# A top-k search by bits: comparison with a constant, update by columns, one more block counted on ScalarE, reciprocals by pairs

## The chip, the cores and the metric

The kernel runs on one core of one Trainium2 chip. The metric is device microseconds from start to end of the program, as the median of repeated runs. PE is TensorE, the matrix engine; PEld is its weight load; DVE is VectorE, ACT is ScalarE, POOL is GpSimd, SP is SyncE, which here issues DMAs. Each engine works off its own instructions in a fixed order, and an instruction that waits for another engine holds up everything behind it on its own.

## The reference, cut to what matters

One decoder layer on 1024 tokens of width 1024, in float32: a feed-forward part (FFN1), a mixer, a second feed-forward part (FFN2), each followed by a LayerNorm. The change lies in the mixer, above all in the choice of the 256 keys of each query:

```python
def block(i):                      # 128 queries, Q_BLOCK * i + 0..127
    causal = key_pos[None, :] <= t[:, None]
    logit = einsum('bqhd,bsd->bqhs', qib, ki_f) * IDX_DIM ** -0.5
    score = einsum('bqh,bqhs->bqs', wib, relu(logit))
    score = where(causal[None], score, -inf)
    _, sel = lax.top_k(score, 256)
    ...
    sc = einsum('bqhc,bqkc->bqhk', qa, c[sel])
    p = softmax(where(valid, sc, -inf), axis=-1)
    o_lat = einsum('bqhk,bqkc->bqhc', p, c[sel])
```

Beside the attention the mixer has a gated MLP (gelu of a projection, a LayerNorm of one half, a 128x128 spatial matrix for each of 8 groups, a product with the other half), and one output projection over both.

## The kernel before

Every product of float32 operands is made of three matmuls: each operand is split into a high part (an ACT copy, L87) and the remainder (a subtraction on DVE or POOL, L88), and `mm3` (L112 to L114) adds high times high, high times low and low times high.

The stages of the mixer, in the order of PE: the projection of the indexer's keys and queries and of a first piece of columns (`piece`, tiles `pN`), with the indexer's scores between them (`scores`, tile `lg`: ACT takes the relu at L758, DVE adds the four heads); two more pieces whose gelus ACT writes into `v` and `u` (L1090, L1096); the gate (`gate`, tile `sv`, DVE L895); transposes of the gated part and its output projection (`wout`, tile `y`); query projections (`queries`, tile `pT`, evacuated by ACT L662, L663 and DVE L664 into `ql`); `q_abs` (tile `qa`, evacuated by L87 on ACT and L88 on DVE, some by L94 and L96); and the attention, block by block of 128 queries: `softmax` (tile `sc`) and, one job later, `attend` (transposes, tile `pT`, tile `ol`).

Which keys are allowed is found for every query without sorting. `topk` finds the 256th largest score of each row bit by bit: 31 steps, each of which sets a trial bit, counts how many scores of the row lie below the trial value, and keeps or drops the bit. Blocks 0 and 1 need no search. A first search runs for blocks 3 and 2 together (two columns in the small tiles), a second one for blocks 7, 5, 4 and 6 (four columns, in this order). In a step, one block's row of scores is counted by one instruction: on ACT (L798, the sign of score minus trial, summed) or on DVE (L789). A comparison of the sums with a row of limits (L801), the next value from the comparison's result (L810) and the next trial bit (L808) follow on DVE, in 128x2 or 128x4 values. The sums on ACT and DVE count differently, so the limits are a small tile with one constant for each column (memsets at L785). In the first search ACT counts block 3 (512 scores) and DVE block 2 (384); in the second ACT counts blocks 7 and 5 (1024 and 768) and DVE blocks 4 and 6 (640 and 896). After the last step come an adjustment of the ACT blocks (L816 to L828, which counts them once on DVE) and, block by block, the mask: ACT counts once more (L839), POOL writes a mask (L844), DVE finds equal scores and their rank (L848 to L854), POOL adds them (L855).

Both searches are generators in a list of background work. `pump(n)` takes n steps of every generator there; the calls stand between the pieces, the projections and the attention's jobs, with the numbers of a table (P0, PX, B, C, Q, W, A). That gives the order of the program; a scheduler of the framework then orders each engine's instructions by a timeline that it estimates itself. `attention` pumps until the mask of a block is there before it begins that block.

`softmax` adds the mask and finds the maximum on DVE (L964, `m`), takes the exponential on ACT (L966), which also sums it into a 128x1 tile `l`, takes the reciprocal on DVE (L967), and multiplies on POOL (L968). Two heads share a tile `p`.

The page of `score` for block 4 (640 of 1024 columns) also holds block 2's 384 columns.

## Time and profile before

| | |
|---|---|
| Median of three runs | 1787.45 us (1786.04, 1787.45, 1789.47) |
| The profiled execution | 1789.27 us, of which the span is 1787.6 us |
| Granted TensorE clock, mean of that execution | 0.989 |
| Busy share of the span: PE, DVE, ACT, POOL | 97%, 74%, 44%, 25% |
| The first search: first and last count on DVE of both searches | 692.9 us, 915.2 us |
| The first and the last softmax reciprocal | 924.4 us, 1059.0 us |

The profile shows one execution, with times in microseconds from the start of the span. "PE busy" counts the stretch of the matmuls at whatever clock was granted, so a stage can be slow either because PE is idle or because its granted clock is below 1.00; the clock has two levels, 1.2 and 2.4 GHz, and a number between stands for a mix of both. A bracket at a row's end, as in [2.71 <-ACT u L1096], is the idle time of that engine before that instruction and what ended it.

### The profile page before, as it was taken

To read this page: it belongs to the slowest core of one execution; us is meant where nothing else is said; L and a number is where in the kernel's file an instruction comes from. 1 tells how busy PE (TensorE), PEld (TensorE's weight loads), DVE (VectorE), ACT (ScalarE), POOL (GpSimd) and SP (SyncE) were. 2 spreads that over 40 slices of the span, in tenths; PEclk is the share of its full clock that TensorE was granted. 3 is DMA by queue.
4 is the path that set the end of the run, shared out by engine and by line. 5 is a ranking of instruction groups with operands and counts; after the bars stand their busy time and mean duration, and the time that the engine had idled before them with its cause. 6 is when DMAs were issued, how large, how long until landed. Compare 5 with 4: busy or idle time off the path is not lost.

```text
span 1787.6 us, 22197 instructions
## 1 busy us (share of the span) xinstructions
PE 1734.7 (97%) x8056; PEld 1457.2 (82%) x8056; DVE 1322.2 (74%) x2186; ACT 787.5 (44%) x1328; POOL 453.0 (25%) x314
## 2 busy tenths in 40 slices
PE   8999999999999999998988999999999999999997
PEld 6878888888888889996867888888788888888886
DVE  5777755666885866899989877878777555589586
ACT  5421322323645336658796662453223222355551
POOL 0003422221000571224247430100323222200036
PEclk9999999999999999999999999999999999999999
DMA  7435432228554331113510005434453322763532
GB/s 284 154 135 200 157 126 88 89 103 310 181 169 138 124 118 43 48 48 103 176 46 25 1 1 195 170 118 169 162 182 119 140 94 89 274 198 124 182 100 83
DMA packets 81789, 235.36 MB, mean 132 GB/s; under 512 B 8208, under 2 KB 8720, under 8 KB 81680
## 3 DMA queue, kind: packets, MB, share of 16 engines
q1 hardware_dynamic: 78320, 225.82, 36.3%
q0 software_dynamic: 1920, 2.89, 0.8%
q10 hardware_dynamic: 1440, 5.24, 0.7%
q8 instruction: 63, 1.03, 0.2%
q14 instruction: 46, 0.38, 0.1%
HBM read 168.64 MB, written 62.39 MB: 129 GB/s over the span
## 4 chain that ended last, share of the span: by engine, by line
PE 82%; DVE 10%; ACT 3%; DMA 2%; issue 1%; POOL 1%; SPq 0%; ACTq 0%; POOLq 0%; DVEq 0%
PE ab L112 15%; PE ab L114 14%; PE ab L113 14%; PE y L112 5%; PE y L114 5%; PE y L113 5%; PE z L114 3%; PE z L112 3%; PE z L113 3%; DMA w<-in_ffn_w_dram 2%; PE tr L977 2%; DVE dve L789 1%; PE pN L112 1%; PE pN L114 1%; PE pN L113 1%
## 5 line engine op out<-in xcount | busy, mean ns | idle before, releaser
L112 PE MATMUL ab<-xs,hi 128*128 128x512 f32 x1232 | 481.7, 391 | 13.1 <-ACT xs L87 5.4
L113 PE MATMUL ab<-xs,hi 128*128 128x512 f32 x1232 | 480.8, 390 | 0.0
L114 PE MATMUL ab<-xs,lo 128*128 128x512 f32 x1232 | 480.6, 390 | 0.0
L112 PEld LDWEIGHTS ab<-xs,hi 128*128 128x128 f32 x1232 | 232.5, 189 | 62.5 <-ACT xs L87 5.4
L88 POOL TENSOR_TENSOR lo<-w,hi 128x1024 fp32r<-128x1024 f32 x54 | 136.8, 2534 | 565.1 <-ACT hi L87 508.0
L113 PEld LDWEIGHTS ab<-xs,hi 128*128 128x128 f32 x1232 | 232.6, 189 | 48.7 <-DVE xs L88 0.4
L114 PEld LDWEIGHTS ab<-xs,lo 128*128 128x128 f32 x1232 | 232.3, 189 | 48.4
L87 ACT ACTIVATE hi<-w 128x1024 fp32r<-128x1024 f32 (+1 forms) x134 | 137.1, 1039 | 184.7 <-DVE w L251 156.2
L88 DVE TENSOR_TENSOR lo<-w,hi 128x1024 fp32r<-128x1024 f32 (+1 forms) x80 | 94.8, 1195 | 42.3 <-ACT hi L87 41.6
L88 DVE TENSOR_TENSOR a<-hid,a 128x512 fp32r<-128x512 f32 x132 | 93.8, 711 | 25.3 <-ACT a L87 25.2
L307 ACT ACTIVATE h<-c 128x512 f32<-128x512 f32 x34 | 21.5, 631 | 202.2 <-DVE c L374 141.3
L87 ACT ACTIVATE a<-hid 128x512 fp32r<-128x512 f32 x132 | 82.0, 621 | 53.0 <-DMA hid<-f 49.8
L798 ACT ACTIVATE act<-score,tk 128x768 int8<-128x768 f32 (+2 forms) x93 | 86.8, 934 | 39.4 <-DVE tk L810 32.7
L88 DVE TENSOR_TENSOR b<-w,b 128x512 fp32r<-128x512 f32 x110 | 77.5, 704 | 34.2 <-ACT b L87 34.1
L113 PE MATMUL y<-b,a 128*128 128x512 f32 x264 | 102.7, 389 | 0.0
L114 PE MATMUL y<-b,a 128*128 128x512 f32 x264 | 102.7, 389 | 0.0
L113 PE MATMUL z<-b,a 128*128 128x512 f32 x264 | 102.7, 389 | 0.0
L114 PE MATMUL z<-b,a 128*128 128x512 f32 x264 | 102.7, 389 | 0.0
L112 PE MATMUL z<-b,a 128*128 128x512 f32 x264 | 102.5, 389 | 0.0
L112 PE MATMUL y<-b,a 128*128 128x512 f32 x264 | 102.0, 389 | 0.0
L551 POOL TENSOR_TENSOR xacc<-xacc,T 128x512 f32<-128x512 f32 x8 | 13.0, 1651 | 333.8 <-DVE T L524 333.8
L87 ACT ACTIVATE b<-w 128x512 fp32r<-128x512 f32 x110 | 68.4, 622 | 51.8 <-PE z L114 38.5
(272 smaller groups left out, 3657.5 us busy)
## 6 DMA issues: line engine op xcount, KB each, us to landing
w<-in_ffn_w_dram SPq DMA_DIRECT2D x110, 512.0 KB, 6.0
hid<-f SPq DMA_DIRECT2D x60, 512.0 KB, 3.7
w<-in_ffn_w_dram SPq DMA_DIRECT2D x22, 1024.0 KB, 11.2
f<-h SPq DMA_DIRECT2D x32, 512.0 KB, 3.4
f<-c SPq DMA_DIRECT2D x22, 512.0 KB, 3.0
xr<-x_spill SPq DMA_DIRECT2D x16, 512.0 KB, 4.9
x_spill<-xr SPq DMA_DIRECT2D x16, 512.0 KB, 2.9
f<-u SPq DMA_DIRECT2D x24, 256.0 KB, 3.7
```

Of the source, the lines that this page charges most:

```text
L87: nc.scalar.activation(hi, src, AF.Copy)
L88: (eng or nc.vector).tensor_tensor(lo, src, hi.bitcast(F32), ALU.subtract)
L112: mm(out, a[0], b[0], start=start, stop=False, skip_group_check=skip)
L113: mm(out, a[0], b[1], start=False, stop=False, skip_group_check=skip)
L114: mm(out, a[1], b[0], start=False, stop=stop, skip_group_check=skip)
L307: nc.scalar.activation(t, c[:, 0], AF.Silu)
L551: nc.gpsimd.tensor_tensor(acc[j][:, HALF:], acc[j][:, HALF:], T[j], ALU.add)
L789: V.tensor_scalar(self.marks("dve", s.shape[-1]), s, f, None, ALU.is_lt, ALU.add, accum_out=val[:, j : j + 1])
L798: nc.scalar.activation(out, s, AF.Sign, bias=fj, scale=-1.0, accum_out=val[:, j : j + 1])
L977: nc.tensor.transpose(pt[:, hh * P : (hh + 1) * P], ps4[hh][:, j * P : (j + 1) * P], self.ident)
```

## The change

- In the first search ACT counts both blocks, and block 2's scores are padded from 384 to 512 columns with -3e38, so that the two sums have the same limit. They lie in the second half of the page of block 3. DVE counts nothing in these steps.
- In the second search ACT still counts blocks 7 and 5, and block 5 is padded from 768 to 1024; DVE counts blocks 4 and 6 as before. DVE's counts begin from a constant that makes their sums comparable with ACT's.
- So there is one limit for all columns, and the comparison (L801, now L799) is a tensor_scalar with an immediate in place of a tensor_tensor with a tile. The tiles of limits and their six memsets are gone; two POOL memsets write the padding.
- The update (L810) was one scalar_tensor_tensor over two or four columns. It is now one tensor_scalar for each column, with the other operand as the column's scalar.
- Reciprocals are taken for two heads at once (128x2), after the second of them, and both heads are then multiplied on POOL one after the other. There are 32 of them in place of 64.

The table of pumps is the same.

```diff
-        dst = self.score[i]
+        dst = self.score[i][:, :s]
...
-    def topk(self, blocks, plan):
+    def topk(self, blocks, n_act):
...
-        for n, thr in zip(range(lo, n_act + 1), limits):
-            for j, i in enumerate(blocks):
-                nc.gpsimd.memset(thr[:, j : j + 1], float((i + 1) * P - (512 if j < n else 256)))
+        limit = float(self.score[blocks[0]].shape[-1] - 512)
 
         def below(f, j):
+
             s = self.score[blocks[j]]
-            V.tensor_scalar(self.marks("dve", s.shape[-1]), s, f, None, ALU.is_lt, ALU.add, accum_out=val[:, j : j + 1])
-
-        def count(f, n):
+            n = s.shape[-1]
+            V.tensor_scalar(self.marks("dve", n), s, f, limit - (n - 256), ALU.is_lt, ALU.add, accum_out=val[:, j : j + 1])
+
+        def count(f):
...
-                if j < n:
+                if j < n_act:
...
-            V.tensor_tensor(di, val, limits[n - lo], ALU.is_gt)
-
-        count(None, plan(31))
+            V.tensor_scalar(di, val, limit, None, ALU.is_gt)
+
+        count(None)
...
-            count(fa, plan(b))
-            V.scalar_tensor_tensor(fb.bitcast(I32), di, b, fni, ALU.logical_shift_left, ALU.bitwise_xor)
+            count(fa)
+            for j in range(w):
+                c = slice(j, j + 1)
+                V.tensor_scalar(fb.bitcast(I32)[:, c], di[:, c], b, fni[:, c], ALU.logical_shift_left, ALU.bitwise_xor)
...
-            if lo < n_act:
-                V.tensor_scalar(val[:, :lo], val[:, :lo], -256.0, None, ALU.add)
-                V.tensor_tensor(di[:, c], val[:, c], limits[0][:, c], ALU.is_le)
-            else:
-                V.tensor_scalar(val[:, c], val[:, c], -256.0, None, ALU.add)
-                V.tensor_tensor(di[:, c], val[:, c], limits[0][:, c], ALU.is_le)
+            V.tensor_scalar(di[:, c], val[:, c], limit, None, ALU.is_le)
...
-        m, l = self.small("m", 1), self.small("l", 1)
+        e = head % 2
+        if e == 0:
+            self.pp, self.sums = self.large("p", (P, 2, 1024), F32), self.small("l", 2)
+        p = self.pp[:, e]
+        m = self.small("m", 1)
...
-        nc.scalar.activation(p, p, AF.Exp, bias=m, scale=-1.0, accum_out=l)
-        V.reciprocal(l, l)
-        self.engine(PAR["PN"][head % 4]).tensor_scalar(p, p, l, 0.0, ALU.mult, ALU.add)
+        nc.scalar.activation(p, p, AF.Exp, bias=m, scale=-1.0, accum_out=self.sums[:, e : e + 1])
+        if e:
+            V.reciprocal(self.sums, self.sums)
+            for j in range(2):
+                x = self.pp[:, j, :s]
+                nc.gpsimd.tensor_scalar(x, x, self.sums[:, j : j + 1], 0.0, ALU.mult, ALU.add)
...
-        self.score = {7: pg[0], 6: pg[1][:, :896], 5: pg[2][:, :768], 4: pg[3][:, :640], 2: pg[3][:, 640:], 3: pg[4][:, :512]}
+        self.score = {7: pg[0], 6: pg[1][:, :896], 5: pg[2], 4: pg[3][:, :640], 2: pg[4][:, HALF:], 3: pg[4][:, :HALF]}
+        for i in (2, 5):
+            nc.gpsimd.memset(self.score[i][:, (i + 1) * P :], -3.0e38)
...
-            self.bg[:] = [self.topk([3, 2], lambda b: PAR["K1"][sum(b < x for x in PAR["K1B"])])]
+            self.bg[:] = [self.topk([3, 2], 2)]
...
-        self.bg.append(self.topk(PAR["KO"], lambda b: PAR["K2"][sum(b < x for x in PAR["K2B"])]))
+        self.bg.append(self.topk(PAR["KO"], 2))
```

The order of the instructions moves with it, at three places. The tiles `tk_...` are the small tiles of a search, and `score_...` is a block's scores; the numbers behind the names only number the tiles.

The first is DVE in the first search, at the end of the indexer's projections. Before, a step is a count of 384, the comparison, the update and the next trial bit:

```order
L808 TENSOR_SCALAR tk_5121<-tk_5117 128x2
L789 TENSOR_SCALAR dve_5207,tk_5116<-score_4749,tk_5117 128x384
L801 TENSOR_TENSOR tk_5119<-tk_5116,tk_5123 128x2
L810 SCALAR_TENSOR_TENSOR tk_5118<-tk_5119,tk_5121 128x2
L808 TENSOR_SCALAR tk_5121<-tk_5118 128x2
```

With the change:

```order
L664 TENSOR_TENSOR qil_4768<-pT_5175,qi_4764 128x512
L799 TENSOR_SCALAR tk_5121<-tk_5118 128x2
L810 TENSOR_SCALAR tk_5120<-tk_5121,tk_5123 128x1 x2
L806 TENSOR_SCALAR tk_5123<-tk_5120 128x2
L799 TENSOR_SCALAR tk_5121<-tk_5118 128x2
```

The count is gone from DVE, and each step is now four small instructions, of which the first waits for two counts on ACT.

The second place is ACT around the gelus of the last piece (`u<-pN`), before the gate. Before, the counts of the two searches (512, and 1024 with 768) stand between the gelus:

```order
L798 ACTIVATE act_6474,tk_5116<-score_4750,tk_5118 128x512
L1096 ACTIVATE u_5585<-pN_6095 128x384
L1096 ACTIVATE u_5586<-pN_6121 128x384
L798 ACTIVATE act_6481,tk_5889<-score_4746,tk_5890 128x1024
L798 ACTIVATE act_6483,tk_5889<-score_4748,tk_5890 128x768
L798 ACTIVATE act_6492,tk_5116<-score_4750,tk_5117 128x512
L1096 ACTIVATE u_5586<-pN_6147 128x384
L798 ACTIVATE act_6499,tk_5889<-score_4746,tk_5891 128x1024
```

With the change:

```order
L1097 ACTIVATE u_5601<-pN_6140 128x384
L796 ACTIVATE act_6509,tk_5905<-score_4746,tk_5906 128x1024
L1097 ACTIVATE u_5601<-pN_6166 128x384
L796 ACTIVATE act_6511,tk_5905<-score_4748,tk_5906 128x1024
L796 ACTIVATE act_6523,tk_5118<-score_4750,tk_5119 128x512
L796 ACTIVATE act_6525,tk_5118<-score_4750,tk_5119 128x512
L796 ACTIVATE act_6531,tk_5905<-score_4746,tk_5907 128x1024
L796 ACTIVATE act_6533,tk_5905<-score_4748,tk_5907 128x1024
L1097 ACTIVATE u_5602<-pN_6240 128x384
```

One gelu stands behind three counts before (1024, 768, 512), and behind five with the change.

The third is DVE where the attention begins. Before, the last step of the second search is over before the first softmax. With the change DVE has there:

```order
L799 TENSOR_SCALAR tk_5908<-tk_5905 128x4
L960 ISA p_7620,m_7629<-sc_7625,bias 128x256
L960 ISA m_7629 128x1
L88 TENSOR_TENSOR act_4481<-qa_7534,act_4480 128x4x128
L810 TENSOR_SCALAR tk_5906<-tk_5908,tk_5910 128x1 x4
L960 ISA p_7681,m_7683<-sc_7677,bias 128x256
L960 ISA m_7683 128x1
L964 RECIPROCAL l_7602<-l_7602 128x2
L787 TENSOR_SCALAR dve_7668,tk_5905<-score_4749,tk_5906 128x640
L960 ISA p_7681,m_7690<-sc_7686,bias 128x256
L960 ISA m_7690 128x1
L806 TENSOR_SCALAR tk_5910<-tk_5906 128x4
```

The steps of the second search now stand among the softmax sums (L960, `m`) and the evacuations of `qa`; ACT has eleven counts of 1024 between the split of `c` into `ch` and the first softmax of block 2, where before it had one count of 768 and four of the masks' counts.

## Rows read from the trace of the kernel before

**Rows 1.** The page: the span, and TensorE's busy time in it.

```profile
span 1787.6 us, 22197 instructions
PE 1734.7 (97%) x8056; PEld 1457.2 (82%) x8056; DVE 1322.2 (74%) x2186; ACT 787.5 (44%) x1328; POOL 453.0 (25%) x314
```

**Rows 2.** Busy time by stretch: length, engines (instructions), PEclk, DMA share, GB/s.

```profile
695.00:760.00 65.00, 64.78 (x356) 62.46 (x355) 56.88 (x144) 44.97 (x102) 16.51 (x15) 1.00 0.21 60
760.00:850.00 90.00, 78.88 (x410) 72.27 (x409) 86.92 (x266) 63.85 (x125) 31.96 (x21) 0.94 0.26 77
850.00:912.00 62.00, 62.00 (x276) 51.31 (x276) 57.00 (x153) 51.21 (x92) 16.60 (x15) 1.00 0.45 150
912.00:967.00 55.00, 45.47 (x236) 35.26 (x235) 48.76 (x156) 44.71 (x116) 35.77 (x41) 0.97 0.05 10
967.00:1000.00 33.00, 27.96 (x147) 24.30 (x146) 30.19 (x53) 19.71 (x39) 23.64 (x16) 0.84 0.09 32
```

**Rows 3.** Timeline of PE: start, length, engine, line, tiles, [idle before].

```profile
793.38 0.39 PE L112 MATMUL sv<-vn,ws 128*128 128x256 f32 x1 [2.71 <-ACT u L1096]
814.90 0.55 PE L112 MATMUL sv<-vn,ws 128*128 128x256 f32 x1 [4.09 <-DVE tk L801]
```

**Rows 4.** Timeline of all engines, 806 to 815 us.

```profile
807.32 4.70 POOL L88 TENSOR_TENSOR wo<-wo,wo 128x1024 fp32r<-128x1024 f32 x2 [23.78 <-ACT wo L87]
...
808.14 1.60 DVE L801 TENSOR_TENSOR tk<-tk,tk 128x4 int32<-128x4 f32 x1 [0.52 <-ACT act L798]
...
809.77 2.28 DVE L810 SCALAR_TENSOR_TENSOR tk<-tk,tk 128x4 int32<-128x4 int32 x1
...
814.14 0.61 DVE L895 SCALAR_TENSOR_TENSOR u<-sv,bs,u 128x128 f32<-128x128 f32 x2
```

**Rows 5.** The search's small tiles `tk`: count, min/median/max ns, first and last start.

```profile
L801 DVE TENSOR_TENSOR tk<-tk,tk x64: 128/161/1599, 692.2 to 912.8; 128x2 int32<-128x2 f32 x32, 128x4 int32<-128x4 f32 x32
L808 DVE TENSOR_SCALAR tk<-tk x62: 138/170/2349, 692.8 to 908.6; 128x2 int32<-128x2 int32 x31, 128x4 int32<-128x4 int32 x31
L810 DVE SCALAR_TENSOR_TENSOR tk<-tk,tk x62: 128/161/2276, 693.9 to 913.0; 128x2 int32<-128x2 int32 x31, 128x4 int32<-128x4 int32 x31
L840 DVE TENSOR_SCALAR tk<-tk x6: 151/154/155, 856.2 to 929.2; 128x1 f32<-128x1 f32 x6
```

**Rows 6.** Timeline of all engines: one step of the first search, alone.

```profile
700.92 0.16 DVE L801 TENSOR_TENSOR tk<-tk,tk 128x2 int32<-128x2 f32 x1 [0.22 <-ACT act L798]
...
701.37 0.72 ACT L798 ACTIVATE act<-score,tk 128x512 int8<-128x512 f32 x1 [0.48 <-DVE tk L810]
701.39 0.61 DVE L789 TENSOR_SCALAR_CACHE_REDUCE dve<-score,tk 128x384 int8<-128x384 f32 x1
...
702.22 0.16 DVE L801 TENSOR_TENSOR tk<-tk,tk 128x2 int32<-128x2 f32 x1 [0.22 <-ACT act L798]
```

**Rows 7.** Timeline of all engines: one step of the second search, with PE full.

```profile
858.88 0.16 DVE L801 TENSOR_TENSOR tk<-tk,tk 128x4 int32<-128x4 f32 x1
...
859.36 0.87 DVE L789 TENSOR_SCALAR_CACHE_REDUCE dve<-score,tk 128x640 int8<-128x640 f32 x1
...
860.27 1.15 DVE L789 TENSOR_SCALAR_CACHE_REDUCE dve<-score,tk 128x896 int8<-128x896 f32 x1
...
861.95 0.16 DVE L801 TENSOR_TENSOR tk<-tk,tk 128x4 int32<-128x4 f32 x1
```

**Rows 8.** Timeline of ACT before the wait at 793.38 us.

```profile
789.80 1.15 ACT L798 ACTIVATE act<-score,tk 128x1024 int8<-128x1024 f32 x1 [2.40 <-DVE tk L810]
...
791.08 0.93 ACT L798 ACTIVATE act<-score,tk 128x768 int8<-128x768 f32 x1
...
792.86 0.47 ACT L1096 ACTIVATE u<-pN 128x384 f32<-128x384 f32 x1
```

**Rows 9.** Busy time of 920 to 940 us, columns as in Rows 2.

```profile
920.00:940.00 20.00, 16.46 (x84) 12.23 (x82) 14.87 (x62) 19.89 (x56) 12.75 (x19) 0.99 0.01 2
```

**Rows 10.** The softmax reciprocals, columns as in Rows 5.

```profile
L967 DVE RECIPROCAL l<-l x64: 131/158/166, 924.4 to 1059.0; 128x1 f32<-128x1 f32 x64
```

11 lines of the change are left out of this document (3 added, 8 removed).

## The prediction

> **What bounds the kernel now.** I read the page first: PE is busy for 1734.7 of 1787.6 us, so at most 53 us of idle time can be won in the whole program [rows 1]. Then I cut the part that the change touches into stretches: 695 to 760 us is the indexer with the first search, 760 to 850 the gelus, the gate and its projection, 850 to 912 the output projection and the last queries, 912 to 967 the query products and the first softmaxes, 967 to 1000 the attention of the next blocks. Before 695 and after the attention nothing changes but two small memsets. The reader should look at PE's busy time against the length [rows 2]: 0.2 us idle in the first stretch, 11.1 in the second, 0.0 in the third, 9.5 in the fourth, 5.0 in the fifth: 25.9 us, about half of the program's idle time. The clock is the second thing to see: 0.94 in the second stretch means 90 x 0.06 = 5.4 us of full-speed time not granted, and 0.84 in the fifth 33 x 0.16 = 5.3 us; both fall where PE had just been idle. Third, who is full there. In the second stretch DVE has 86.9 of 90 us: it is the bound. In the fourth it has 48.8 of 55 and ACT 44.7 of 55, and from 920 to 940 us ACT has 19.9 of 20 while PE has 16.5 [rows 9].
>
> The two largest waits of PE in the second stretch show two different causes [rows 3]. At 814.90 it waited 4.09 us for DVE, which had sat in a comparison of 1.60 us and an update of 2.28 us, each with four values a row, while POOL ran two subtractions for 4.70 us [rows 4]; the sum that PE wanted (L895) stood behind them. At 793.38 it waited 2.71 us for a gelu on ACT, which stood behind counts of 1024, 768 and 512 columns begun at 789.80; the gelu began at 792.86, so the three took 3.06 us [rows 8].
>
> **The search's steps, one by one.** The comparison, the trial bit and the update each have a median near 0.16 us, and each has a longest instance of 1.60 to 2.35 us [rows 5]. A column of the new update is a 128x1 tensor_scalar; the nearest row is L840, 151 to 155 ns in six of six [rows 5]. An added column costs between nothing, if it overlaps the one before, and 0.15 us: 0 to 0.15 a step in the first search, 0 to 0.45 in the second. I take half of each, 0.08 and 0.23, since the columns don't depend on each other.
>
> One step of the first search alone takes 702.22 - 700.92 = 1.30 us, with 0.85 from the start of ACT's count to the next comparison [rows 6]. With both counts on ACT the step becomes 1.30 + 0.72 to 0.85 + 0.08, about 2.1 to 2.2 us. A step of the second takes 861.95 - 858.88 = 3.07 us, of which DVE's two counts are 0.87 and 1.15 [rows 7]; ACT's count of block 5 grows by 1.15 - 0.93 = 0.22 us [rows 8], so about 3.5 us. The searches thus end later: by 31 x 0.85 = 26 us and 31 x 0.45 = 14 us if nothing else lay between the steps. In the order of the changed kernel it is the second search's last five steps that now stand among the softmaxes.
>
> In work: DVE loses 32 counts of 384, 32 x 0.61 = 19.5 us [rows 6], and 32 reciprocals, 32 x 0.16 = 5 us at most [rows 10], and gains 31 x 0.31 = 9.6 us of columns. The steps issue no DMAs. ACT gains 32 counts of 512, 32 x 0.72 to 0.85 = 23 to 27 us, and 31 x 0.22 = 7 us. What counts is where these fall.
>
> **695 to 760 us.** Some 17 counts move to ACT: 45.0 + 17 x 0.85 = 59.4 of 65 us. DVE falls by 17 x 0.61 = 10 us. PE is idle for only 0.2 us [rows 2]: nothing to win, but the relus of the scores now queue behind twice as many counts, and DVE's comparison waits for two counts instead of one, with evacuations of the projections (L664) behind it. Cost +1, between 0 and +4 (a quarter of the 14.4 us added to ACT).
>
> **760 to 850 us.** By the order, DVE has here 13 counts of the first search less (13 x 0.61 = 8 us), three first-search steps less (3 x 0.5 = 1.5) and one or two second-search steps less (about 3.5), against columns for 10 and 11 steps (10 x 0.08 + 11 x 0.23 = 3.3): 86.9 falls to about 77 of 90. Where DVE ends PE's wait, the wait shrinks. Of the 4.09 us, the two long instances hold 1.60 + 2.28 - 2 x 0.16 = 3.56 us [rows 4]: -3.6 if they go. Of the other 11.1 - 4.1 - 2.7 = 4.3 us of idle I take about half, -2, and of the clock's 5.4 us -2, for idle time that no longer precedes it. Against it, one gelu now has five counts ahead of it: 3.06 + 0.72 + 0.22 + 1.15 = 5.2 us, if they are released together; I take +1. Sum -6.6, say -6.5; between -14 (all idle time, and over half of the clock) and -3 (only the small waits).
>
> Whether the long instances go is the open point. What the rows show is that L801 and L810, with two tiles of several columns as inputs, and also L808, with one, were each held once for 1.6 to 2.35 us, and that L840 with one column never was [rows 5]. The Trainium skill ("SBUF — State Buffer", section "Who interferes with whom") says that a DVE instruction with two SBUF inputs waits for a GpSimd instruction that reads SBUF, and that a tensor_scalar can do so too where it enters a two-port mode. The trace agrees for L801 and L810 beside POOL's 4.70 us. By that rule the columns are free, but the new comparison, a tensor_scalar over two or four values as L808 is, may still be held; that is the third rival. The other way, the skill's "VectorE: DVE Perf Modes", section "Rules for kernel authors", advises to minimize the number of DVE instructions, against an update by columns. By that rule each column would count in full, at the 0.15 us of its row: from 760 to 850 us 10 x 0.07 + 11 x 0.22 = 3 us more than I take, and a sum of 1792.5.
>
> **850 to 912 us.** PE is full and both others have room (57.0 and 51.2 of 62) [rows 2]. 0.
>
> **912 to 967 us.** The search's last five steps have moved in here. ACT has, by the order, eleven counts of 1024 before the first softmax of block 2, 11 x 1.15 = 12.7 us, where it had one of 768 and four counts of masks (640 to 1024 columns, 0.83, 0.93, 1.04 and 1.15 us between the lengths of [rows 6, 8]), together 4.9 us: +8; the four masks follow later. ACT's free time from 912 to 967 is 55 - 44.7 = 10.3 us, but none of it lies between 920 and 940 [rows 9], which is where PE waits. On DVE five steps of 0.87 + 1.15 + 0.7 are 14 us, less the two counts of the adjustment that move on and eight reciprocals, about +10: 48.8 + 10 = 59 of 55. So DVE alone gives +4, ACT alone up to +8, and both waiting for each other up to +12. I take +8, the amount by which the full engine is loaded more.
>
> **967 to 1000 us.** Fifteen reciprocals become seven: about -1.3 us of DVE's 30.2. The first head's multiplication waits for the second head's exponential, but its transposes come one job later, which covers that; without the cover it costs one exponential. Against that, masks that come later. -0.5, between -3 and +1.
>
> **Sum.** -6.5 + 1 + 0 + 8 - 0.5 = +2. On the profiled execution, 1789.27 us (span 1787.6 and 1.7 around it), that is 1791.3. That execution is 1.8 us above the median of 1787.45, so the median becomes 1789.5 us.
>
> **The rivals.**
> 1. Faster: the gate gets all its idle time back and the attention absorbs the steps. For it: DVE is the bound from 760 to 850 and loses 10 us, and the scheduler has spread the late steps among the softmaxes, with other work between a count and its comparison. Against it: ACT full from 920 to 940. -11 + 0 + 3 - 1 = -9: 1778.5 us.
> 2. Slower: ScalarE becomes the bound. It takes 30 to 34 us more, and it already ends PE's wait at 793.38. Place: the gelus ahead of the gate, and the evacuations of `qa` and exponentials behind eleven counts. Price: -4 + 4 + 12 = +12: 1799.5 us. It decides as soon as ACT stays full past 940, since the free 10.3 us are then used up by the added 8 and the masks.
> 3. The change doesn't do what it says: the long instances move from the update to the comparison or the trial bit. L808's 2349 ns speaks for it [rows 5]. The 3.6 us stay: -3 + 1 + 8 - 0.5 = +5.5: 1793 us.
>
> **How the numbers follow.** About 0.2% of the time, 3.6 us, can be told from no change: 1783.9 to 1791.0 counts as the same. The forecast has a chance of 0.40 (0.22 within, 0.13 slower, 0.05 faster by its spread of some 4 us), rival 1 0.29 (0.28 faster, 0.01 within), rival 2 0.18 (slower), rival 3 0.13 (0.08 slower, 0.05 within). Faster 0.33, same 0.28, slower 0.39. The likeliest case's own range is 1785 to 1794; to hold 8 in 10 it reaches to rival 1 and to rival 2: 1778 to 1801.
>
> **What would show it.** Right: PE's wait near 814.90 under 1 us, and PE from 760 to 850 with about 84 of 90 us worth of today's work; ACT from 695 to 760 near 59 us; the first reciprocals' stretch about 8 us longer, with PE waiting for `m`, `qa` or exponentials behind counts. Wrong: an update column over 0.3 us beside POOL, or comparisons of 1 us and more (rival 3); PE's idle time after 912 no larger than 9.5 us (rival 1); a wait for a gelu of over 4 us (rival 2). The prediction fails most easily at the +8: it takes a full engine's added work as time, while the scheduler may have put it in gaps.

## The result and the profile after

The changed kernel takes 1801.95 us (four runs, 1801.15 to 1802.56) against 1787.58 us: a ratio of 1.0080, 95% interval 1.0062 to 1.0097, so 14.4 us slower. The forecast was 1789.5 us, the range 1778 to 1801: the size is that of rival 2, and just outside the range. The profiled execution after took 1801.15 us with a span of 1799.4; the one before had 1787.6, so the traces hold 11.8 us of the difference (the execution before was 1.7 us above this median, the one after 0.8 below its own).

The page, its span and its busy time, to be read against [rows 1]:

```profile
span 1799.4 us, 22262 instructions
PE 1738.0 (97%) x8056; PEld 1457.7 (81%) x8056; DVE 1320.4 (73%) x2214; ACT 817.2 (45%) x1392; POOL 451.3 (25%) x310
```

DVE lost 1.8 us in all, though 32 counts and 32 reciprocals are gone; ACT gained 29.7. The two together have 27.9 us more to do. The stretches, with the columns of [rows 2]:

```profile
695.00:760.00 65.00, 63.72 (x352) 61.83 (x352) 46.40 (x129) 56.14 (x134) 16.67 (x15) 1.00 0.20 55
760.00:850.00 90.00, 82.88 (x426) 75.32 (x425) 80.81 (x270) 70.42 (x136) 30.50 (x20) 0.94 0.29 91
850.00:912.00 62.00, 57.64 (x258) 47.28 (x256) 57.71 (x177) 48.36 (x84) 17.87 (x15) 0.99 0.42 132
912.00:967.00 55.00, 40.37 (x179) 30.56 (x180) 52.44 (x167) 47.82 (x118) 27.57 (x32) 0.88 0.03 6
967.00:1000.00 33.00, 27.33 (x150) 23.48 (x148) 27.05 (x50) 20.27 (x41) 25.45 (x21) 0.90 0.10 33
```

From 760 to 850 us PE gained: 82.9 of 90 against 78.9. From 850 on it lost: 57.6 of 62 against 62.0, and 40.4 of 55 at a clock of 0.88 against 45.5 at 0.97. Stretches by the clock mix work that has shifted, so here is the time by the work, from the first matmul of one kind to the first of the next, with the idle time of PE inside it:

| From, to | Before: us (idle) | After: us (idle) | Difference | Forecast |
|---|---|---|---|---|
| start to the first scores (`lg`) | 676.9 | 673.6 | -3.3 | none |
| first `lg` to first gate (`sv`) | 112.6 (0.8) | 114.1 (2.1) | +1.5 | +1 |
| first `sv` to first `y` | 54.9 (9.4) | 51.0 (5.5) | -3.8 | -6.5 |
| first `y` to first `qa` | 68.2 (1.7) | 69.6 (2.9) | +1.4 | 0 |
| first `qa` to first `sc` of 512 columns | 33.0 (7.6) | 42.5 (13.9) | +9.5 | +8 |
| to the last `sc` of 320 columns (block 4) | 57.0 (6.8) | 61.2 (11.6) | +4.2 | -0.5 |
| to the last `sc` of 512 columns | 52.6 (0.0) | 54.6 (0.0) | +2.0 | 0 |

With +0.4 behind them these make 11.9 us. So the gain and the loss were placed rightly as far as the first softmaxes, and what came behind them was missed. Two things about the rows. The last two belong together: with the change the first of them holds 259 matmuls where it held 272, and the second 310 where it held 298, so the +2.0, without idle time and at a clock of 1.00, is work that changed rows, and the pair makes +6.2. And a row of one execution is good to some 3 us: e13 below, the same instructions in another order and no slower, has +3.5 in the row from `qa`.

In the row from `qa`, idle time is 6.3 of the 9.5 us. The rest passes with PE busy at a lower granted clock. First the kernel before, then the changed one, columns as in [rows 2]:

```profile
912.51:945.49 32.98, 25.27 (x121) 18.64 (x119) 27.38 (x95) 28.75 (x75) 17.16 (x24) 0.95 0.06 13
```

```profile
908.29:950.77 42.48, 28.51 (x119) 21.60 (x119) 39.76 (x132) 39.08 (x94) 16.81 (x26) 0.84 0.06 13
```

With the change the clock stands at 1.2 GHz there from 911.3 to 918.2 and from 942.1 to 948.9 us, and each spell begins inside a wait of PE, of 3.85 and 2.81 us; before, there was one such spell of 3.4 us. At the gate the mean is 0.91 before and 0.90 after.

The waits of PE, in the timeline's columns as in [rows 3]:

```profile
791.12 0.39 PE L112 MATMUL sv<-vn,ws 128*128 128x256 f32 x1 [2.27 <-ACT u L1097]
...
810.32 0.36 PE L112 MATMUL sv<-vn,ws 128*128 128x256 f32 x1 [2.38 <-DVE u L890]
...
908.29 0.73 PE L672 MATMUL qa<-q,wuk 128*128 128x512 f32 x2 [1.38 <-DVE ql L664]
912.87 1.22 PE L672 MATMUL qa<-q,wuk 128*128 128x512 f32 x2 [3.85 <-DVE ql L664]
...
943.10 0.80 PE L112 MATMUL ol<-pT,ch 128*128 128x512 f32 x1 [2.81 <-ACT pT L87]
...
987.47 0.50 PE L113 MATMUL ol<-pT,ch 128*128 128x512 f32 x1 [2.69 <-DVE pT L88]
...
1003.53 0.63 PE L112 MATMUL sc<-cTh,act 128*128 128x320 f32 x1 [2.27 <-DVE m L960]
```

The wait of 4.09 us at the gate has become 2.38. The rest stands later: for the last query's remainder, for an evacuation that ACT makes behind a count (943.10), for one that DVE makes behind a search for equal scores (987.47), and for a softmax behind a rank scan at 1003 us. Two of these kinds of wait were there before:

```profile
915.31 0.73 PE L672 MATMUL qa<-q,wuk 128*128 128x512 f32 x2 [2.09 <-DVE ql L664]
...
992.70 0.64 PE L112 MATMUL sc<-cTh,act 128*128 128x320 f32 x1 [2.27 <-DVE m L964]
```

The one at 1003 us is no longer than it was, and a query's remainder is waited for 5.27 us in e13 too. The search before the wait at 987.47 took 3.67 us beside POOL; before, the same search of 896 columns took 0.67, but the next one, of 1024, took 2.80 beside POOL's subtractions, and takes 0.72 now. These are rows of DVE and POOL after, then of DVE before:

```profile
983.15 3.67 DVE L843 TENSOR_SCALAR eq<-score,tk 128x896 bf16<-128x896 f32 x1
980.06 4.73 POOL L88 TENSOR_TENSOR wo<-wo,wo 128x1024 fp32r<-128x1024 f32 x2
```

```profile
970.01 0.67 DVE L848 TENSOR_SCALAR eq<-score,tk 128x896 bf16<-128x896 f32 x1
...
973.87 2.80 DVE L848 TENSOR_SCALAR eq<-score,tk 128x1024 bf16<-128x1024 f32 x1
```

The small instructions of the search, as in [rows 5]:

```profile
L810 DVE TENSOR_SCALAR tk<-tk,tk x186: 171/205/221, 689.4 to 946.1; 128x1 int32<-128x1 int32 x186
...
L799 DVE TENSOR_SCALAR tk<-tk x64: 145/170/2379, 686.8 to 944.7; 128x2 int32<-128x2 f32 x32, 128x4 int32<-128x4 f32 x32
L806 DVE TENSOR_SCALAR tk<-tk x62: 152/169/1904, 687.4 to 942.9; 128x2 int32<-128x2 int32 x31, 128x4 int32<-128x4 int32 x31
```

No column was ever held; the comparison and the trial bit were. At the very place of [rows 4], beside the same two subtractions on POOL (these are timeline rows of DVE, then POOL):

```profile
804.97 2.38 DVE L799 TENSOR_SCALAR tk<-tk 128x2 int32<-128x2 f32 x1
807.39 0.34 DVE L810 TENSOR_SCALAR tk<-tk,tk 128x1 int32<-128x1 int32 x2
807.76 1.90 DVE L806 TENSOR_SCALAR tk<-tk 128x2 int32<-128x2 int32 x1
```

```profile
804.94 4.70 POOL L88 TENSOR_TENSOR wo<-wo,wo 128x1024 fp32r<-128x1024 f32 x2 [24.83 <-ACT wo L87]
```

Added up over the search, what these instructions took beyond 0.17 us each, counted where it was over 0.12 us, is 20.6 us before and 16.2 after. The Trainium skill ("SBUF — State Buffer", section "Who interferes with whom") lists tensor_scalar among the instructions that can enter a two-port mode and then wait for GpSimd. The trace agrees for two and four values; for one value no run shows a hold.

Each step also became longer. One step of the first search alone, in the timelines of DVE and ACT, to set beside [rows 6]:

```profile
696.47 0.39 DVE L799 TENSOR_SCALAR tk<-tk 128x2 int32<-128x2 f32 x1 [1.74 <-ACT act L796]
...
698.89 0.17 DVE L799 TENSOR_SCALAR tk<-tk 128x2 int32<-128x2 f32 x1 [1.47 <-ACT act L796]
```

```profile
697.20 0.72 ACT L796 ACTIVATE act<-score,tk 128x512 int8<-128x512 f32 x1 [0.76 <-DVE tk L810]
...
698.04 0.72 ACT L796 ACTIVATE act<-score,tk 128x512 int8<-128x512 f32 x1
```

It takes 2.42 us where it took 1.30; the comparison at its start was itself 0.22 us longer than usual beside a subtraction, so a step without that is 2.20, within the 2.1 to 2.2 us forecast. Two columns take 0.34 us in one go, four take 0.58 (at 873.95 us): the columns follow one another at 0.12 to 0.17 us and do not overlap.

### The profile page after: what moved, and what is told of

Same layout as the page of the kernel before. It is cut to its first block, busy times and chain, and to the rows that moved or that the text cites. A ratio compares the mean times of both kernels' runs of the same rounds, so it can differ in the third digit from the quotient of the medians.

```text
span 1799.4 us, 22262 instructions
## 1 busy us (share of the span) xinstructions
PE 1738.0 (97%) x8056; PEld 1457.7 (81%) x8056; DVE 1320.4 (73%) x2214; ACT 817.2 (45%) x1392; POOL 451.3 (25%) x310
## 3 DMA queue, kind: packets, MB, share of 16 engines
q10 hardware_dynamic: 1440, 5.24, 0.7%
## 4 chain that ended last, share of the span: by engine, by line
PE 80%; DVE 10%; ACT 3%; DMA 3%; issue 2%; POOL 1%; SPq 0%; POOLq 0%; ACTq 0%; DVEq 0%
PE ab L112 14%; PE ab L114 14%; PE ab L113 14%; PE y L112 5%; PE y L113 5%; PE y L114 5%; PE z L113 3%; PE z L112 3%; PE z L114 3%; DMA w<-in_ffn_w_dram 2%; PE tr L976 1%; ACT act L796 1%; PE pN L114 1%; PE pN L112 1%; PE pN L113 1%
## 5 line engine op out<-in xcount | busy, mean ns | idle before, releaser
L796 ACT ACTIVATE act<-score,tk 128x512 int8<-128x512 f32 (+1 forms) x124 | 115.8, 934 | 33.2 <-DVE tk L810 24.0
```

Source lines behind the costliest of these rows:

```text
L796: nc.scalar.activation(out, s, AF.Sign, bias=fj, scale=-1.0, accum_out=val[:, j : j + 1])
```

## The experiments

All ratios are to runs of the kernel before on the same chip. The groups ran on different chips; the median of the kernel before was 1787.6 to 1789.1 us there.

### One edit alone

e1: ScalarE counts one block more, the rest as before:

```diff
-'K1': [1, 1], 'K1B': [4]
+'K1': [2], 'K1B': []
```

> The kernel before, with one edit: ScalarE counts block 2 too in the first search (384 columns, unpadded; still one update and a tile of limits). Theory A, that ScalarE's extra counts make the searches late and hold the attention, expects most of the loss here: 1796 to 1802 us. Theory B, that the update by columns lengthens each step of the second search and pushes its last steps into the attention, expects no loss, 1782 to 1789 us, with the first product for the gate's output projection earlier than at 849 us and the last softmax sum near 1055 us.

Measured: 1796.17 us, ratio 1.0042 (1.0029 to 1.0055), 7.5 us. It costs alone, and at places of the kind that the prediction named: PE waits 2.73 us for a gelu at 751 us behind relus and counts, and 5.24 us for a query's remainder at 920 (though e13, no slower, waits as long for one). The time is just inside theory A's range; theory B expected none of this.

e2: the update by columns alone:

```diff
-            V.scalar_tensor_tensor(fb.bitcast(I32), di, b, fni, ALU.logical_shift_left, ALU.bitwise_xor)
+            for j in range(w):
+                c = slice(j, j + 1)
+                V.tensor_scalar(fb.bitcast(I32)[:, c], di[:, c], b, fni[:, c], ALU.logical_shift_left, ALU.bitwise_xor)
```

> The kernel before, with one edit: the update as one tensor_scalar for each column. Theory A expects 1785 to 1790 us, since nothing moves to ScalarE. Theory B expects a loss from this edit alone, 1793 to 1799 us: two steps of the second search stand behind the first softmax in its order, and 31 x 0.42 us of columns lie in the chain of the second search.

Measured: 1793.89 us, ratio 1.0032 (1.0019 to 1.0045), 5.7 us; theory A fell here as far as it was to be the only cause. The rows of its small instructions (L812 is the column, L808 the trial bit):

```profile
L812 DVE TENSOR_SCALAR tk<-tk,tk x186: 177/206/241, 692.8 to 936.2; 128x1 int32<-128x1 int32 x186
...
L808 DVE TENSOR_SCALAR tk<-tk x62: 155/169/2267, 691.7 to 928.8; 128x2 int32<-128x2 int32 x31, 128x4 int32<-128x4 int32 x31
```

The update is never held, but the trial bit right behind it is held 11 times for 14.9 us in all, where before it was twice for 2.5; with the comparison the sum is 22.7 us against 20.6. The holds were handed on, not removed: rival 3 of the prediction.

e3: the pair reciprocals alone (the change in `softmax`):

```diff
-        V.reciprocal(l, l)
-        self.engine(PAR["PN"][head % 4]).tensor_scalar(p, p, l, 0.0, ALU.mult, ALU.add)
+        if e:
+            V.reciprocal(self.sums, self.sums)
+            for j in range(2):
+                x = self.pp[:, j, :s]
+                nc.gpsimd.tensor_scalar(x, x, self.sums[:, j : j + 1], 0.0, ALU.mult, ALU.add)
```

> The kernel before, with one edit: reciprocals of two heads at once, and both heads multiplied after the second. Theories A and B both expect no difference, 1785 to 1790 us. Theory C, that the first head's multiplication waits for the second head's exponential and so holds up transposes and POOL's masks, expects 1792 us or more, with the loss after 960 us.

Measured: 1792.30 us, ratio 1.0022 (1.0010 to 1.0033), 3.9 us: theory C's size, after 967 us as it said. In the timelines of DVE, POOL and PE:

```profile
973.37 4.26 DVE L850 TENSOR_TENSOR_SCAN rank<-eq 128x896 f32<-128x896 bf16 x1
977.55 2.76 DVE L848 TENSOR_SCALAR eq<-score,tk 128x1024 bf16<-128x1024 f32 x1
```

```profile
973.34 6.42 POOL L88 TENSOR_TENSOR wo<-wo,wo 128x1024 fp32r<-128x1024 f32 x2
```

```profile
980.96 0.80 PE L113 MATMUL ol<-pT,ch 128*128 128x512 f32 x1 [4.89 <-DVE pT L88]
```

The scan of 896 columns, 2.02 us in the trace of before, runs beside POOL's subtractions and takes 4.26; the evacuation that PE wants stands behind it and the next search for equal scores.

e7: what is left of the change without these three, the comparison with a constant and the padding. It is the changed kernel with the old update, the old `softmax` and

```diff
-            self.bg[:] = [self.topk([3, 2], 2)]
+            self.bg[:] = [self.topk([3, 2], 1)]
```

> The changed kernel with ScalarE counting one block in the first search again, one update for all columns, and a reciprocal for each head: what is left is the comparison with a constant and the padding it needs (block 5 counted over 1024). The single edits cost 7.7 us (ScalarE's extra block), 5.4 (columns) and 3.8 (reciprocals), together 17 where the whole change costs 14.4. Theory D, that the costs add, expects 1784 to 1787 us here. Theory E, that they overlap because all of them delay the same attention, expects no gain, 1788 to 1793 us.

Measured: 1792.29 us, ratio 1.0029 (1.0018 to 1.0039), 5.2 us. That the costs simply add is thereby wrong: the four singles make 22 us, the whole 14.4. Theory D fell, and the time is in theory E's range. Its profiled execution was its fastest; up to the last `ol` it is 1.0 us ahead, after being 3.4 ahead at the first scores, before any search, so where the loss falls stays open.

### Edits together

e8: ScalarE's block and the constant; the changed kernel with the old `softmax` and the old update:

```diff
-                V.tensor_scalar(fb.bitcast(I32)[:, c], di[:, c], b, fni[:, c], ALU.logical_shift_left, ALU.bitwise_xor)
+            V.scalar_tensor_tensor(fb.bitcast(I32), di, b, fni, ALU.logical_shift_left, ALU.bitwise_xor)
...
-            V.reciprocal(self.sums, self.sums)
+        V.reciprocal(l, l)
```

> The changed kernel with one update for all columns and a reciprocal for each head: ScalarE counts both blocks, comparison with a constant. Theory D (costs add) expects 1792 to 1796 us. Theory E expects 1797 us or more, since ScalarE's counts alone already fill the start of the attention.

Measured: 1795.78 us, ratio 1.0045 (1.0030 to 1.0060), 8.0 us: hardly more than the first of its two parts alone (7.5). It lies in theory D's range (1792 to 1796), but by e7's 5.2 the sum of the two parts would be 12.7.

e5: the changed kernel with one update again:

```diff
-            for j in range(w):
-                c = slice(j, j + 1)
-                V.tensor_scalar(fb.bitcast(I32)[:, c], di[:, c], b, fni[:, c], ALU.logical_shift_left, ALU.bitwise_xor)
+            V.scalar_tensor_tensor(fb.bitcast(I32), di, b, fni, ALU.logical_shift_left, ALU.bitwise_xor)
```

> The changed kernel, with one edit undone: the update is again one scalar_tensor_tensor over all columns. Theory A expects the loss to stay, 1798 to 1802 us. Theory B expects most of it to go, 1784 to 1791 us: no step of the second search stands behind the first softmax in its order. Theory C expects 1797 us or more.

Measured: 1798.77 us, ratio 1.0054 (1.0036 to 1.0072): by the ratios 4.7 us of the loss go and 9.7 stay, though the two intervals overlap. The median lies inside the ranges of theories A (1798 to 1802) and C; theory B (most goes) fell.

e4: the changed kernel with DVE counting block 2 again:

```diff
-[self.topk([3, 2], 2)]
+[self.topk([3, 2], 1)]
```

> The changed kernel, with one edit undone: DVE counts block 2 in the first search again. Theory A (ScalarE's counts are most of the loss) expects 1787 to 1791 us. Theory D expects 14.4 - 7.7 = 6.7 above the kernel before, 1793 to 1797 us.

Measured: 1801.28 us, ratio 1.0081 (1.0064 to 1.0098). Nothing goes: DVE gets back what ScalarE loses. Theory A fell for good, and theory D (1793 to 1797 us) too.

e6: the changed kernel with a reciprocal for each head:

```diff
-        if e:
-            V.reciprocal(self.sums, self.sums)
+        V.reciprocal(l, l)
```

> The changed kernel, with one edit undone: a reciprocal for each head again. Theory D expects 14.4 - 3.8 = 10.6 above the kernel before, 1796 to 1800 us, with the gain after 960 us. If the reciprocals cost only where POOL's work happens to meet the rank scans, 1800 to 1803 us is as possible.

Measured: 1801.36 us, ratio 1.0077 (1.0062 to 1.0092): nothing that can be told from no change, as the second of the two expectations had it (1800 to 1803 us). In the whole change the reciprocals are not what costs.

### How late the second search ends

e9: five steps more in the kernel before, which change no bit:

```diff
+        for _ in range(5 if 7 in blocks else 0):
+            V.tensor_scalar(fni, fa.bitcast(I32), 0, None, ALU.bitwise_xor)
+            count(fa, plan(0))
+            V.scalar_tensor_tensor(fb.bitcast(I32), di, 0, fni, ALU.bitwise_and, ALU.bitwise_xor)
+            fa, fb = fb, fa
+            yield
```

> The kernel before, with five more steps in the second search that change no bit (their result is masked off). Nothing else of the change is in it. Theory F, that the end of the second search sets the time, because the masks of blocks 4 to 7 then fall into the attention, expects a loss much like the whole change's: 1795 to 1802 us, with the last count of 640 columns near 935 us in place of 908.7. If the place of each edit matters and not the search's end, the added steps sit in free time and the kernel stays at 1787 to 1791 us.

Measured: 1791.52 us, ratio 1.0015 (1.0006 to 1.0025), 2.7 us. Theory F fell: the last count of 640 columns starts at 939.8 us, as late as in the changed kernel (942.1, before 908.7), and the last mask is written later still. First the changed kernel's row of POOL, then this one's:

```profile
1008.14 2.14 POOL L850 TENSOR_TENSOR bias<-bias,eq 128x1024 bf16<-128x1024 bf16 x1 [1.16 <-DVE eq L849]
```

```profile
1025.55 2.14 POOL L861 TENSOR_TENSOR bias<-bias,eq 128x1024 bf16<-128x1024 bf16 x1 [1.75 <-DVE l L973]
```

In the kernel before, so late an end of the search costs 2.7 us, work included, and not 14; the other expectation (1787 to 1791 us) is missed by half a microsecond.

e10: five steps less in the changed kernel:

```diff
-        for b in range(30, -1, -1):
+        for b in range(30, 4 if 7 in blocks else -1, -1):
```

> The changed kernel, with the last five of 31 steps of the second search left out (the five lowest bits of the limits of blocks 4 to 7 aren't searched). ScalarE's counts, the columns and the reciprocals are all as changed. Theory F expects most of the loss to go: 1787 to 1793 us. If the edits cost where they stand, only the work of five steps goes, and the kernel stays at 1797 to 1801 us.

Measured: 1788.87 us, ratio 1.0001 (0.9991 to 1.0010). The whole loss goes, as theory F expected and against the other expectation (1797 to 1801 us). Its page, in busy time:

```profile
PE 1736.3 (97%) x8056; PEld 1456.2 (81%) x8056; DVE 1305.5 (73%) x2164; ACT 806.3 (45%) x1372; POOL 457.0 (26%) x310
```

Against the changed kernel ACT has 10.9 us less to do and DVE 14.9 less, so lateness and work go together here, and e9 and e10 do not decide theory F between them. By the rows of the table above and against the kernel before, the gate's stretch gains 2.3 us, the one from `qa` to the 512-column `sc` still loses 6.9, but the next two together gain 5.1.

### Other places for the same steps

To tell whether the table of pumps is made for the old order, e13 has the last two columns of the second search exchanged in the kernel before:

```diff
-'KO': [7, 5, 4, 6]
+'KO': [7, 5, 6, 4]
```

> The kernel before, with the last two columns of the second search exchanged (blocks 7, 5, 6, 4 in place of 7, 5, 4, 6): the same instructions, in a slightly other order. Theory H, that much of each single edit's cost is that of an order which the pump table was not made for, expects 1790 to 1794 us. Theory A to F's common ground, that the instructions cost, expects 1787 to 1789.5 us.

Measured: 1787.57 us, ratio 1.0003 (0.9993 to 1.0012). Another order of the same instructions costs nothing here; theory H lost its first leg.

e14 is the changed kernel, and e16 the kernel before, with more steps before 850 us:

```diff
-'B': [0, 0, 0, 0, 0, 0, 0, 2], 'C': [0, 1, 0, 0, 0, 0, 1, 0]
+'B': [0, 0, 1, 1, 1, 1, 1, 2], 'C': [0, 1, 1, 1, 1, 1, 1, 1]
```

> The changed kernel with another table of pumps: 0, 0, 1, 1, 1, 1, 1, 2 after the tiles of the second piece (before 0 seven times and 2) and 0, 1, 1, 1, 1, 1, 1, 1 after those of the third (before 0, 1, 0, 0, 0, 0, 1, 0). All instructions are as changed. In its order no step of the second search and no count of the masks stands behind the first exponential. Theory H expects most of the loss to go, 1783 to 1792 us. If the instructions themselves cost, ScalarE is only full earlier, before the gate, and the kernel stays at 1797 us or more.

> The kernel before with the pumps of e14. If a gain of e14 belongs to the table alone, this gains as much against 1787.5 us. Theory H expects a loss or no change here, 1788 to 1795 us: the table was made for the kernel before, and DVE has no room from 760 to 850 us (86.9 of 90 us).

Measured: 1816.49 us, ratio 1.0162 (1.0147 to 1.0178), and 1802.86 us, ratio 1.0091 (1.0071 to 1.0110): both lose some 15 us more, and the distance between them stays at 13.6. Theory H's ranges are missed by both. The waits of PE, first of the changed kernel with these pumps, then of the kernel before with them:

```profile
862.35 0.80 PE L112 MATMUL y<-wo,gmh 128*128 128x512 f32 x1 [16.57 <-DVE ql L664]
...
925.81 0.80 PE L112 MATMUL pT<-act,wT 128*128 128x512 f32 x1 [16.79 <-ACT yf L919]
```

```profile
850.25 0.79 PE L112 MATMUL y<-wo,gmh 128*128 128x512 f32 x1 [6.01 <-DVE ql L664]
...
908.88 0.80 PE L112 MATMUL pT<-act,wT 128*128 128x512 f32 x1 [12.73 <-ACT yf L924]
```

The attention's part of the table above, from the first `qa` to the last `sc` of 320 columns, falls from 103.7 to 78.9 us in the one and from 90.0 to 81.6 in the other; the output projection and the queries pay more than that back. e15, the changed kernel with a third table, does the same in a smaller way:

```diff
-'B': [0, 0, 0, 0, 0, 0, 0, 2]
+'B': [0, 0, 1, 1, 2, 2, 2, 2]
```

> The changed kernel with a third table: 0, 0, 1, 1, 2, 2, 2, 2 after the tiles of the second piece, the third piece as before. The steps are pulled forward further still, into the stretch before 790 us. Theory H expects 1783 to 1792 us, like e14. If ScalarE's counts hold the gelus of the second piece, 1795 us or more.

Measured: 1805.19 us, ratio 1.0097 (1.0081 to 1.0113). With all three tables the changed kernel's steps cost, in one stage or another, and theory H's forecasts fell. But e14's table costs the kernel before 16 us as well, so these tables are bad in themselves; whether a table made for the changed kernel takes the loss back was not tried.

### The same work, with nobody waiting for it

e17: the kernel before with the columns added behind its one update, into a tile not read in the search:

```diff
             V.scalar_tensor_tensor(fb.bitcast(I32), di, b, fni, ALU.logical_shift_left, ALU.bitwise_xor)
+            for j in range(w):
+                c = slice(j, j + 1)
+                V.tensor_scalar(need.bitcast(I32)[:, c], di[:, c], b, fni[:, c], ALU.logical_shift_left, ALU.bitwise_xor)
```

> The kernel before, with the column instructions of e2 added behind its one update, writing to a tile that nobody reads in the search. ScalarE's next count doesn't wait for them; DVE's own counts stand behind them. If DVE's time is the price, it costs as much as the columns themselves or more (one update of 0.16 us stays): 1793 to 1797 us. If the price is ScalarE's wait for the update, 1787 to 1790 us.

Measured: 1798.02 us, ratio 1.0047 (1.0032 to 1.0061), 8.4 us, for 20.3 us more of DVE's busy time: just above the first expectation (1793 to 1797), and against the second.

e18: the kernel before with a count of block 2 on ACT that nobody reads:

```diff
+            if 3 in blocks:
+                s = self.score[2]
+                nc.scalar.activation(self.marks("act", s.shape[-1]), s, AF.Sign, bias=0.0 if f is None else f[:, 1:2], scale=-1.0, accum_out=need[:, 1:2])
             V.tensor_tensor(di, val, limits[n - lo], ALU.is_gt)
```

> The kernel before, with ScalarE also counting block 2 (384 columns) in each step of the first search, into a sum that nobody reads; DVE counts it as before, and the comparison doesn't wait for ScalarE's second count. If ScalarE's time is the price, it costs as much as e1 or more, since DVE gains nothing: 1794 to 1800 us. If the price in e1 is the longer step of the first search, 1787 to 1791 us.

Measured: 1791.49 us, ratio 1.0020 (1.0010 to 1.0030), 3.6 us, for 19.6 us more of ACT: between the two expectations, near the second. The two kernels' busy time:

```profile
PE 1734.3 (97%) x8056; PEld 1454.2 (81%) x8056; DVE 1342.5 (75%) x2372; ACT 786.4 (44%) x1328; POOL 449.9 (25%) x314
```

```profile
PE 1735.1 (97%) x8056; PEld 1455.1 (81%) x8056; DVE 1324.3 (74%) x2186; ACT 807.1 (45%) x1392; POOL 453.2 (25%) x314
```

So DVE's time is a price by itself, 0.41 us for each us. ScalarE's is about 0.18 us for each; that is half of what ScalarE's extra block costs in e1 (7.5 us, with 20.5 us more of ACT and 20.2 less of DVE). What else differs in e1 is the step, in which the comparison waits for two counts; the other half was not separated further.

### POOL's subtractions left out

In e11 the weights of the output projection get zeros for their low part from a POOL memset, in place of the subtraction; e12 has the pair reciprocals of e3 too:

```diff
-        return [self.load_w(self.ins["w_out"][part * 4 + k], "wo", eng=self.nc.gpsimd, page=k >= pages) for k in range(4)]
+        two = []
+        for k in range(4):
+            ...
+            self.nc.scalar.activation(hi, raw, AF.Copy)
+            self.nc.gpsimd.memset(lo.bitcast(F32), 0.0)
+            two.append((hi, lo))
+        return two
```

> The kernel before, with POOL's subtractions for the output projection's weights left out (eight L88 on POOL; a POOL memset writes zeros in place of the low part of these weights). It is the base for the next kernel. Theory G, that POOL's subtractions hold DVE's scans and small search instructions, expects the comparison and the update near 808 us without long instances and 1780 to 1786 us.

> The same kernel without these subtractions, with the pair reciprocals added. Theory G, that the pair reciprocals cost 3.8 us only because a rank scan then meets POOL's subtractions near 973 us, expects no difference to the kernel without subtractions, within 1.5 us. If the later first multiplication itself costs, the difference stays near 4 us.

Measured: 1781.71 us, ratio 0.9962 (0.9948 to 0.9977), and 1785.04 us, ratio 0.9983 (0.9974 to 0.9992). The eight subtractions cost 6.8 us, more than DVE's busy time shows (6.2 us less): PE's wait of 4.09 us for DVE at the gate is gone (the one for a gelu is 4.06 in place of 2.71), and the stretch from the first `sc` of 512 columns to the last of 320 falls from 57.0 to 49.3 us. The comparison and the update near 807 us take 0.17 and 0.16 us there, and the search of 1024 columns 0.73 in place of 2.80, so theory G holds for the subtractions. But the pair reciprocals still cost 3.3 us without them, against its forecast. This does not rule out the meeting with POOL: e12's search of 896 columns is held all the same, beside the memsets that stand in for the subtractions. The rows are e12's, DVE then POOL, then e11's of DVE:

```profile
967.31 3.14 DVE L848 TENSOR_SCALAR eq<-score,tk 128x896 bf16<-128x896 f32 x1
967.23 2.74 POOL L916 MEMSET wo<- 128x1024 f32 x3
```

```profile
967.90 0.67 DVE L848 TENSOR_SCALAR eq<-score,tk 128x896 bf16<-128x896 f32 x1
```

So why the reciprocals cost in e3 and e12 stays open; that they change which of DVE's instructions meet POOL's work is likely, and not shown.

## Why the prediction was wrong

**The term for 967 to 1000 us, -0.5, is the step that failed.** By the work it is +4.2 us, and +2.0 to the last softmax sums, +6.2 together: 6.7 us of the 12.4 by which the time was missed. All but 1.4 of it is idle time of PE (+4.8); the granted clock did not change (0.91 and 0.92 in the first of the two rows). The prediction had the late masks in one clause ("Against that, masks that come later") and gave them no price. The last mask came 11 us later (997.2 to 1008.1 us), and rank scans, searches for equal scores and evacuations now met in a stretch where the trace of before had DVE busy for 30.2 of 33 us [rows 2]. The longest of the new waits, 2.69 us at 987.47, stands behind the search that took 3.67 us beside POOL. e6, with its last mask at 1007.5 us and the same search at 4.60, loses 5.3 us in this stretch too, and e10, with the last mask at 984.9, gains there. That lateness is the mechanism is not shown: e9 has the same late end of the search and a later last mask, and loses only 2.7 us in all; e4, e5 and e8, with last masks at 1001.5 to 1003.4, are at +0.2, +0.5 and -0.5 us in this stretch and still lose 8.0 to 14.5 us. So the step failed in its size, for a wait that it had at nothing; the cause of the size stays open.

**912 to 967 us, +8.** The place and the size were right: +9.5 us. Of the mechanism, a full engine's added work, two thirds are there as idle time of PE (+6.3); the rest is the clock, 0.84 in place of 0.95, for which the sum had no term, so part of the agreement is luck. e2, e4 to e8 and e10, each with the columns or the constant, lose 4.5 to 8.7 us in this stretch (e2 with 18 matmuls more in it); e1, e9, e13 and e18, with neither, 3.2 to 4.3, but e3 0.1, and e17, with added columns, 1.9. The price of the whole was rival 2's (+12), its place partly: the evacuations of `qa`, as it said; but the longest waits are for a query's remainder (3.85 us) and for transposes (2.81), which it did not name; and not the gelus ahead of the gate, for which PE waits 2.27 us where it waited 2.71.

**760 to 850 us, -6.5.** It was -3.8. The idle time fell by 3.9 us, near the 4.6 of the sum. Most of the miss is the term of the clock, -2: the granted clock is 0.94 from 760 to 850 us in both [rows 2]; the two waits that are left, of 2.27 and 2.38 us, are each followed by a spell at 1.2 GHz (791.9 to 798.7 and 812.4 to 815.8 us). Within the idle time two more sizes were off. The 3.6 us of the long instances did not go: 2.38 us of comparison and 1.90 of trial bit stand where 1.60 and 2.28 stood, though PE's wait there shrank all the same. That is rival 3, to which I gave 0.13, though the trial bit's 2349 ns in [rows 5] was the direct row for it (the prediction took each of the three as held once; in the trace it was 6 comparisons, 7 updates and 2 trial bits, 20.6 us in all): a tensor_scalar with two or four values is held like the others, and both new neighbours of the update are such. And an added column costs 0.12 to 0.17 us, not half of it: L840, to which I bounded it, was the right price in full. In e2 all this shows as a sum of holds that rises from 20.6 to 22.7 us. The Trainium skill's rule to minimize the number of DVE instructions ("VectorE: DVE Perf Modes", section "Rules for kernel authors") agrees with e2 and e17, where more of them on DVE cost 5.7 and 8.4 us.

**850 to 912 us, 0.** It was +1.4: PE came 5.6 us earlier to the output projection and 4.2 us earlier to `qa`, and its idle time in between rose from 1.7 to 2.9 us (1.38 of it ahead of the first `qa`, for a query's remainder; the 3.85 at 912.87 falls in the next row). A part of the gate's gain was thus given back at the next place where both engines were full.

**695 to 760 us, +1**, was +1.5, with ACT at 56.1 of the 59.4 us forecast. The 3.3 us before the first scores were not forecast. The other kernels reach this point between 0.2 us later and 3.5 us earlier than the profiled execution before, some without any of the change (e16: 2.5 earlier), so most of it belongs to no edit. In the execution before, the granted clock stood at 1.2 GHz for 3.4 us at 33.1 and again at 128.7; in the one after it was 1.00 all the way to the first scores. So from there on the changed kernel's trace has lost 15.2 us.

**How the chances stood.** Of the signs, rival 3's came (comparisons of 1 us and more), rival 2's did not (no wait of over 4 us for a gelu), and the wait at the gate did not fall under 1 us, though the price was nearest to rival 2's. ScalarE was named there as the loser of the change, but it isn't alone: putting its block back (e4) changes nothing, since DVE then has it. What most runs with the same pumps fit, roughly, is the work of both engines together:

| Kernel | DVE + ACT busy, against before | Time, against before |
|---|---|---|
| e13 swapped columns | 0.0 | +0.5 |
| e10 after, five steps less | +2.1 | +0.2 |
| e7 constant | +7.5 | +5.2 |
| e2 columns | +11.4 | +5.7 |
| e5, e8 after, less one and two edits | +13.1, +13.6 | +9.7, +8.0 |
| e17, e18 idle work | +19.2, +21.7 | +8.4, +3.6 |
| e4, e6 after, less one edit | +23.5, +29.7 | +14.5, +13.8 |
| after | +27.9 | +14.4 |
| e1 ScalarE's block, e3 reciprocals | +0.3, +1.0 | +7.5, +3.9 |
| e9 five steps more | +17.8 | +2.7 |

About half a microsecond is lost for each added; the last two lines don't fit, and e18 no better than e9. The runs without the subtractions, e11 and e12, have -6.4 and -7.6 us for -6.8 and -3.0, with less on POOL too. So this is a fit with exceptions, not a cause shown. In e1 work moved between the engines and every step grew; in e3 and e9 the trace does not settle it. The prediction had the numbers for this sum: DVE -24.5 and +9.6, ACT +30 to +34, so +15 to +19, and half of that is +8 to +10. It took each stage's fuller engine instead, and so let a stage with room on one engine count as free. The sum itself was short by 9 to 13 us, all of it on DVE, which was to lose 14.9 us and lost 1.8.

## What to carry to other kernels

Where two engines hand a long chain of small steps to and fro beside the main work, add up the work of both, and ask what half of the added sum would cost (the rough price here, with exceptions), before sorting it by stages: moving a step from one engine to the other, or to another stage, moved the waits here and did not remove them. Before an instruction is rewritten because another engine holds it, look at its neighbours in the chain: if they can be held too, the hold goes to them. And give a thing that comes later (here the masks) a price at the place where it then falls.

## What the runs showed of the hardware

A tensor_scalar with one value a partition was held in none of 372 instances (at most 241 ns; after and e2), of which 83 began while POOL was at work and 35 beside one of its two-input instructions; one with two or four values took up to 2379 ns beside POOL. One value is not enough for a tensor_tensor: one of 128x1 took 1657 ns in e4. Four columns with one value each, independent of one another, take 0.58 us. Leaving out POOL's eight subtractions of 128x1024, none of which is on the profile's critical chain in the mixer's part from 780 to 1010 us, saved 6.8 us (e11); with them went PE's waits of 4.09 us at the gate and of 2.27 us at 992.70, behind instructions of DVE that ran beside them. Memsets on POOL held a tensor_scalar too: the search of 896 columns took 3.14 us beside three of them (e12), and 0.67 in e11.
